# Every third weight unit gets its low part from an accumulating DMA instead of a VectorE subtraction

## The chip, the cores and the metric

The kernel runs on one core of a Trainium2 chip. The metric is the device time in microseconds of one execution; lower is better. Of the kernel before there are three runs, with a median of 2090.06 us (2090.04 to 2090.12).

## The reference

A two-layer decoder trunk on 256 tokens of 2048 features, all in float32. Layer 0 mixes by causal pooling, layer 1 by dilated attention; each is followed by a gated convolutional FFN of width 5504 and by layer norms. Cut to what matters here, it is a long row of matrix products with large weights and few tokens:

```python
# layer 0
p = h @ w_in                                  # 2048 x 2048
mixed = einsum('bsgc,gcd->bsgd', pooled, w_grp) * scale
h = layer_norm(ALPHA * h + mixed @ w_out)
h = layer_norm(ALPHA * h + conv_ffn(h))       # w_up 2048 x 11008, w_down 5504 x 2048
# layer 1
k, v, q = h @ w_k, h @ w_v, h @ w_q           # 2048 x 2048 each
h = layer_norm(ALPHA * h + attention(q, k, v) @ w_o)
h = layer_norm(ALPHA * h + conv_ffn(h))
```

## The kernel before

Each float32 weight is used as the sum of two numbers of a shorter format (float32r, which TensorE multiplies faster): a high part, the weight rounded, and a low part, the weight less its high part. The activations are split in the same way. A product is then w_high x_high + w_high x_low + w_low x_high, three products that TensorE sums in PSUM.

The weights are cut into 364 **units**, blocks of up to 512 rows by 512 columns, which lie in SBUF as 128 partitions x 2048 floats (1 MiB); 24 units of the FFNs have 384 columns or 384 rows. The list `units` sets the order of everything: `run_units` takes one unit after the other, emits its products, and before them calls `ahead(i)`, which issues loads up to unit i + 5 and splits up to unit i + 3. So a unit is split three units before TensorE uses it.

A unit goes through three kinds of buffers:

- `raw`, three buffers: the weights as SP's DMA queue loads them (line 68). The buffers turn round, so unit i uses buffer i mod 3. SP takes its queue in order, and a load waits until its buffer is free.
- `wh`, four buffers: the high part, written by ScalarE (line 76).
- `wl`, four buffers: the low part, written by VectorE as raw less wh (line 77).

The `wh` and `wl` of unit i + 4 can be written when TensorE is done with unit i. The products that read them stand at lines 135 and 136 (a mode with both halves of a PSUM bank), 138 to 140 (a mode with one half) and 164 to 166 (tokens on the partitions). ScalarE and VectorE also carry the products out of PSUM and do the convolution, the gating, the attention's softmax and the norms; their instructions run in the order in which the program emits them. GpSimd (POOL) has almost nothing to do: some memsets, the DMAs of the small constants (lines 792 to 798) at about 26 to 35 us, and three iotas for the attention's masks.

The first four units are split piece by piece, as their rows arrive.

Of the kernel before, what the change touches and what calls it, by code (L numbers as in the profile page):

```python
# [12 lines left out]
AF = mybir.ActivationFunctionType  # L13
OP = mybir.AluOpType
# [18 lines left out]
def trunk(ctx: ExitStack, tc: tile.TileContext, x, pool_w_in, pool_w_grp, pool_scale, pool_w_out,  # L33
          attn_w_q, attn_w_o, shared_w_k, shared_w_v, ffn_w_up, ffn_conv_w, ffn_conv_b, ffn_w_down,
          ln1_g, ln1_b, ln2_g, ln2_b, out):
    nc = tc.nc
    V, A, PE = nc.vector, nc.scalar, nc.tensor
# [10 lines left out]
    def bank(nm):  # L48
        return psp.tile([P, 512], F32, name=nm, tag="ps")

# [1 line left out]
    units = []  # L52
    state = {"loaded": 0, "split": 0, "done": 0}
    raw, wh, wl = {}, {}, {}
    pending, before = [], {}

    def pieces(i, nk):
        return [slice(k, k + 1) for k in range(nk)] if i < 4 else [slice(0, nk)]
# [11 lines left out]
    def do_split(i):  # L70
        r = raw.pop(i)
        shape = [P, r.shape[1], r.shape[2]]
        wh[i] = wp.tile(shape, F32R, name=f"wh{i}", tag="wh")
        wl[i] = wp.tile(shape, F32R, name=f"wl{i}", tag="wl")
        for j, s in enumerate(pieces(i, r.shape[1])):
            A.copy(wh[i][:, s], r[:, s])  # L76
            V.tensor_tensor(wl[i][:, s], r[:, s], wh[i][:, s].bitcast(F32), OP.subtract)  # L77
            if i == 0 and j == 0:
                x_quad(0, (1,))
# [32 lines left out]
                post()  # L112
            state["done"] += 1

# [1 line left out]
    # "ab": w xl beside the rest, in the second half of the bank; "a": all in the first half;  # L116
    # "x": two more columns, the products with the next norm's scale and shift
    XW = T + 2

    def mm_quad(xq, ps, first, last, mode, mid, shifted):  # L120
# [31 lines left out]
                          mm_quad(xqs[j], ps, j == 0, last, mode, mids[j] if j < len(mids) else None, shifted),  # L152
                          (lambda: post(ps)) if last else None))

    # the same product with tokens on the partitions; apart: all of the first 128 tokens first
    def group_tm(w, r0s, c0, ncol, xqs, post, apart=False):
        ps, held = [], []

# [58 lines left out]
    xsrcs = [lambda j=j: XC[j] for j in range(4)]  # L217
    psrcs = [lambda j=j: XP[j] for j in range(4)]

# [1 line left out]
    # d = residual sum less an estimate of its mean; the first product after the norm takes g*d in place of  # L221
    # the norm's result ("x" mode) and is corrected for mean and deviation as it leaves PSUM
    def resid_add(c, first):
        def post(ps):
            for m in range(4):
                y = H[c][:, m, :]
                if first:
                    V.scalar_tensor_tensor(y, y, ALPHA, ps[m][:, :T], op0=OP.mult, op1=OP.add)
                else:
                    V.tensor_tensor(y, y, ps[m][:, :T], OP.add)  # L230
            for m in range(4):
                y = H[c][:, m, :]
                V.tensor_tensor(y, y, ps[m][:, T:], OP.add)
        return post
# [132 lines left out]
                later(2 + q, lambda q=q: norm(q + 1))  # L367
            later(3 + q, lambda q=q: lo(q))

    # a group in "x" mode: (acc - mean * w g) * rstd + w b into dst(m)  # L370
    def norm_evac(ps, nb, tmp, dst):
        wgb = lnp.tile([P, 4, 2], F32, name="wgb", tag="wgb", bufs=2)
        for m in range(nb):
            A.copy(wgb[:, m, :], ps[m][:, T:XW])
        for m0 in range(0, nb, 2):
            ts = [(m, tmp()) for m in range(m0, min(nb, m0 + 2))]
            for m, t in ts:
                V.tensor_tensor(t, ps[m][:, :T], ST["rs"], OP.mult)
            for m, t in ts:
                V.scalar_tensor_tensor(t, ST["mr"], wgb[:, m, 0:1], t, op0=OP.mult, op1=OP.subtract)  # L380
                A.activation(dst(m), t, AF.Identity, scale=-1.0, bias=wgb[:, m, 1:2])

    # the first two column groups of a product take turns, so that its last rows are needed later
    def turns(mark, n):
        a, b = units[mark:mark + n], units[mark + n:mark + 2 * n]
        units[mark:mark + 2 * n] = a[:n - 1] + b[:1] + a[n - 1:] + b[1:]
# [6 lines left out]
        for c in range(4):  # L393
            group(w, rows, 512 * c, 512, srcs, resid_last(c, first, lay, which, after), mode="a", shifted=c > 0 and not first)

    # ================= layer 0, pooling mixer =================
    PADW = 16
    pooled_q, mixed_q = {}, {}

# [39 lines left out]
    def x_quad(q, halves=(0, 1)):  # L439
        xin = XIN  # L440
        if halves[0] == 0:
            H[q] = hp.tile([P, 4, T], F32, name="h", tag="h")
            XC[q] = quad_tile("xc")
        for half in halves:
            ps = bank("xT")
            for kk in range(2):
                for t in range(2):
                    k = 2 * half + kk
                    PE.transpose(ps[:, kk * T + t * P:kk * T + t * P + P], xin[q, t][:, k * P:(k + 1) * P], ident)
            pv2 = ps.rearrange("p (k t) -> p k t", k=2)  # L450
            s = slice(2 * half, 2 * half + 2)
            A.copy(XC[q][:, s, 0, :T], pv2)
            V.tensor_tensor(XC[q][:, s, 1, :T], pv2, XC[q][:, s, 0, :T].bitcast(F32), OP.subtract)
            before.setdefault(min(q + 1, 3), []).append(lambda s=s, pv2=pv2: A.copy(H[q][:, s, :], pv2))
# [22 lines left out]
    units.extend([outs[2], outs[4], outs[3]] + outs[5:])  # L477
    marks.append(len(units))

    # ================= FFN =================  # L480
    def ffn(lay):
        w_up, w_dn = ffn_w_up[lay], ffn_w_down[lay]
        gq, gates = {}, {}
# [101 lines left out]
                up(q)  # L585
            down(range(a, b), b == 11)

# [1 line left out]
    HT = {}  # L589

    def to_tokens(q):
# [54 lines left out]
    ffn(0)  # L646
    marks.append(len(units))

    # ================= layer 1, dilated attention =================
    scale = 1.0 / math.sqrt(P)  # L650
    qk, pr, oq, pT, vts = {}, {}, {}, {}, {}

# [92 lines left out]
    ffn(1)  # L745
    marks.append(len(units))

    # ================= the program =================
    with tc.tile_pool(name="start", bufs=1) as stp:
        for q in range(NQ):  # L750
            for t in range(2):
                XIN[q, t] = stp.tile([P, 512], F32, name=f"xin{q}{t}")
            halves = [slice(0, 256), slice(256, 512)] if q == 0 else [slice(0, 512)]
            for i, h in enumerate(halves):
                for t in range(2):
                    nc.sync.dma_start(XIN[q, t][:, h], x[0, t * P:(t + 1) * P, 512 * q:512 * q + 512][:, h])
                if q == 0:
                    do_load(0, i)
            if q in (1, 2):
                do_load(q)  # L760
            if q < 3:
                state["loaded"] = q + 1
            if q == 0:
                make_identity(nc, ident)
                V.memset(one1, 1.0)
                # the tensor engine's clock rises only under load: keep it busy until the first data is there
                warm = bank("warm")
                for i in range(WARM):
                    PE.matmul(warm[:, :P], one1, one1, start=True, stop=True)
        V.memset(ones, 1.0 / D)  # L770
        A.activation(neg1, one1[0:1, :], AF.Copy, scale=-1.0)
        A.activation(ones4, one1, AF.Copy, scale=4.0 / D)
        V.memset(epst, EPS)
        for c in range(16):
            nc.gpsimd.memset(inv[:, :, c:c + 1], 1.0 / (c + 1))
        x_quad(0, (0,))
        warm = bank("warm")
        for i in range(WARM2):
            PE.matmul(warm[:, :P], one1, one1, start=True, stop=True)

        run_units(3)
    with tc.tile_pool(name="pool", bufs=1) as pp:
# [5 lines left out]
        for l in range(2):  # L788
            n = 80 if l == 0 else 64
            r = pp.tile([80, P], F32, name=f"vrow{l}")  # L790
# [33 lines left out]
    with tc.tile_pool(name="ffn0", bufs=4) as fp:  # L824
        pools["ffn"] = fp

        # how many branches hold a (query, key) pair: keys 0-127 of both query tiles, keys 128-255 of the second
        def masks(i):
            dist = fp.tile([P, P], F32, name="dist", tag="dist", bufs=1)
            nc.gpsimd.iota(dist, pattern=[[-1, P]], base=P * (i == 1), channel_multiplier=1,  # L830
                           allow_small_or_imprecise_dtypes=True)
            idist = fp.tile([P, P], I32, name="idist", tag="idist", bufs=1)
            im = fp.tile([P, P], I32, name="im", tag="im", bufs=1)
            fm = fp.tile([P, P], F32, name="fm", tag="fm", bufs=1)
            cn = cnt[:, i, :]
            V.tensor_copy(idist, dist)
            V.tensor_scalar(cn, dist, float(P), None, op0=OP.is_le)
            for dil in (4, 16):
                V.tensor_scalar(im, idist, dil - 1, None, op0=OP.bitwise_and)
                V.tensor_copy(fm, im)  # L840
                V.scalar_tensor_tensor(cn, fm, 0.0, cn, op0=OP.is_equal, op1=OP.add)
            V.scalar_tensor_tensor(cn, dist, 0.0, cn, op0=OP.is_ge, op1=OP.mult)
            V.tensor_scalar(negm[:, i, :], cn, 0.0, NEG, op0=OP.is_equal, op1=OP.mult)

        for i in range(3):
            later(30 + 2 * i, lambda i=i: masks(i))
        run_units(marks[1])
# [35 lines left out]
```

## Time and profile before

| | |
|---|---|
| median of three runs | 2090.06 us |
| span of the profiled execution | 2086.0 us |
| difference of the two | 4.06 us |
| TensorE busy | 2071.3 us |
| VectorE busy, of it low parts (line 77) | 1393.2 us, 821.9 us |
| ScalarE busy, of it high parts (line 76) | 1030.2 us, 685.7 us |
| bytes read from HBM | 380.01 MB |

The profiled execution's own time is its span; the runs' times also hold the few microseconds around it. In the profile PE is TensorE's products, PEld its loads of weights into the array, DVE is VectorE, ACT is ScalarE, POOL is GpSimd and SP is the engine that issues the loads; SPq and POOLq are the queues that issue DMAs. A row of a group gives line, engine, operation, what is written and read, how many instructions, their busy time and mean duration, and the idle time of the engine just before them with what ended it. A row of the waits gives who waited for whom: total, times, longest. A row of stretches gives the stretch and its length, the busy time of PE, PEld, DVE, ACT and POOL with the instructions in parentheses, the granted clock of TensorE, the share of the DMA engines' time that was busy, and GB/s. An issue row gives the size of one transfer and the median time from issue to landing.

### The profile page before, as it was taken

To read this page: it belongs to the slowest core of one execution; us is meant where nothing else is said; L and a number is where in the kernel's file an instruction comes from. 1 tells how busy PE (TensorE), PEld (TensorE's weight loads), DVE (VectorE), ACT (ScalarE), POOL (GpSimd) and SP (SyncE) were. 2 spreads that over 40 slices of the span, in tenths; PEclk is the share of its full clock that TensorE was granted. 3 is DMA by queue.
4 is the path that set the end of the run, shared out by engine and by line. 5 is a ranking of instruction groups with operands and counts; after the bars stand their busy time and mean duration, and the time that the engine had idled before them with its cause. 6 is when DMAs were issued, how large, how long until landed. Compare 5 with 4: busy or idle time off the path is not lost.

```text
span 2086.0 us, 30530 instructions
## 1 busy us (share of the span) xinstructions
PE 2071.3 (99%) x12959; PEld 1862.8 (89%) x12959; DVE 1393.2 (67%) x1706; ACT 1030.2 (49%) x1146; POOL 11.4 (1%) x38
## 2 busy tenths in 40 slices
PE   9999999999999999999999999999999999999997
PEld 9999998888888888899888889999888888888886
DVE  6757787757756766767855666677646664675676
ACT  6445665345534535546634444476535543544553
POOL 2000000000000000000000000000000000000000
PEclk9999999999999999999999999999999999999999
DMA  8655465555555555554545445545555555555453
GB/s 265 212 187 188 148 212 174 201 184 191 172 200 186 178 202 172 188 186 143 201 161 182 161 162 182 185 159 194 190 184 187 195 182 192 191 182 188 165 197 136
DMA packets 195304, 384.09 MB, mean 184 GB/s; under 512 B 7022, under 2 KB 15876, under 8 KB 194912
## 3 DMA queue, kind: packets, MB, share of 16 engines
q1 hardware_dynamic: 194240, 381.71, 53.8%
q8 instruction: 101, 1.65, 0.3%
q0 software_dynamic: 928, 0.44, 0.1%
q14 instruction: 35, 0.29, 0.0%
HBM read 380.01 MB, written 2.10 MB: 183 GB/s over the span
## 4 chain that ended last, share of the span: by engine, by line
PE 99%; DVE 0%; DMA 0%; SPq 0%; issue 0%; DVEq 0%; ACT 0%
PE acc L135 35%; PE acc L136 18%; PE acc L138 9%; PE acc L139 9%; PE acc L140 9%; PE t L164 5%; PE t L166 5%; PE t L165 5%; PE s L693 0%; PE o L733 0%; DMA xin<-in_x_dram 0%; DVE ht L633 0%; PE pT L720 0%; PE acc L142 0%; PE o L734 0%; PE s L692 0%
## 5 line engine op out<-in xcount | busy, mean ns | idle before, releaser
L77 DVE TENSOR_TENSOR wl<-raw,wh 128x2048 fp32r<-128x2048 f32 (+2 forms) x376 | 821.9, 2188 | 537.0 <-ACT wh L76 526.0
L76 ACT CAST wh<-raw 128x2048 fp32r<-128x2048 f32 (+2 forms) x376 | 685.7, 1827 | 612.8 <-PE acc L135 297.8
L135 PE MATMUL acc<-xc,wh 128*128 128x512 f32 x2624 | 924.1, 396 | 0.0
L136 PE MATMUL acc<-xc,wl 128*128 128x256 f32 x2624 | 737.4, 281 | 0.0
L135 PEld LDWEIGHTS acc<-xc,wh 128*128 128x128 f32 x2624 | 495.3, 189 | 115.9
L136 PEld LDWEIGHTS acc<-xc,wl 128*128 128x128 f32 x2624 | 495.7, 189 | 0.2
L135 PE MATMUL acc<-g,wh 128*128 128x512 f32 x512 | 179.9, 396 | 0.0
L138 PE MATMUL acc<-xc,wh 128*128 128x256 f32 x512 | 144.8, 283 | 1.1 <-ACT wh L76 1.1
L140 PE MATMUL acc<-xc,wl 128*128 128x256 f32 x512 | 144.6, 282 | 0.2 <-DVE wl L77 0.2
L139 PE MATMUL acc<-xc,wh 128*128 128x256 f32 x512 | 144.3, 282 | 0.0
L136 PE MATMUL acc<-g,wl 128*128 128x256 f32 x512 | 143.8, 281 | 0.0
L518 DVE SCALAR_TENSOR_TENSOR c<-u,cv,c 128x256 f32<-128x256 f32 x344 | 141.9, 479 | 0.7
L164 PE MATMUL t<-wh,g 128*128 128x512 f32 x344 | 136.2, 396 | 0.0
L165 PE MATMUL t<-wl,g 128*128 128x512 f32 x344 | 135.6, 394 | 0.0
L166 PE MATMUL t<-wh,g 128*128 128x512 f32 x344 | 135.5, 394 | 0.0
L135 PEld LDWEIGHTS acc<-g,wh 128*128 128x128 f32 x512 | 96.7, 189 | 22.7
L139 PE MATMUL acc<-xp,wh 128*128 128x258 f32 x384 | 109.3, 285 | 0.0
L138 PE MATMUL acc<-xp,wh 128*128 128x258 f32 x384 | 109.2, 284 | 0.0
L140 PE MATMUL acc<-xp,wl 128*128 128x258 f32 x384 | 108.1, 281 | 0.0
L505 ACT COPY ut<-acc 128x256 f32<-128x256 f32 x140 | 51.6, 372 | 96.3 <-PE acc L136 96.1
L138 PEld LDWEIGHTS acc<-xc,wh 128*128 128x128 f32 x512 | 97.3, 190 | 1.3 <-ACT wh L76 1.3
L140 PEld LDWEIGHTS acc<-xc,wl 128*128 128x128 f32 x512 | 96.5, 189 | 0.5 <-DVE wl L77 0.4
(192 smaller groups left out, 2810.7 us busy)
## 6 DMA issues: line engine op xcount, KB each, us to landing
raw<-in_ffn_w_up_dram SPq DMA_DIRECT2D x160, 1024.0 KB, 4.8
raw<-in_ffn_w_down_dram SPq DMA_DIRECT2D x80, 1024.0 KB, 5.0
raw<-in_pool_w_out_dram SPq DMA_DIRECT2D x16, 1024.0 KB, 5.0
raw<-in_shared_w_k_dram SPq DMA_DIRECT2D x16, 1024.0 KB, 4.9
raw<-in_attn_w_q_dram SPq DMA_DIRECT2D x16, 1024.0 KB, 5.0
raw<-in_shared_w_v_dram SPq DMA_DIRECT2D x16, 1024.0 KB, 5.0
raw<-in_attn_w_o_dram SPq DMA_DIRECT2D x16, 1024.0 KB, 5.0
raw<-in_pool_w_in_dram SPq DMA_DIRECT2D x12, 1024.0 KB, 5.4
```

The lines of the kernel that those rows point to most:

```text
L76: A.copy(wh[i][:, s], r[:, s])
L77: V.tensor_tensor(wl[i][:, s], r[:, s], wh[i][:, s].bitcast(F32), OP.subtract)
L135: PE.matmul(ps[m], h[:, k, c], q[:, k, :, :T], start=st, stop=False)
L136: PE.matmul(ps[m][:, :T], l[:, k, c], q[:, k, 0, :T], start=False, stop=sp)
L138: PE.matmul(ps[m][:, :n], h[:, k, c], q[:, k, 0, :n], start=st, stop=False)
L139: PE.matmul(ps[m][:, :n], h[:, k, c], q[:, k, 1, :n], start=False, stop=False)
L140: PE.matmul(ps[m][:, :n], l[:, k, c], q[:, k, 0, :n], start=False, stop=sp and not shifted)
L164: PE.matmul(ps[t], xh, h[:, k, :], start=j == 0 and k == 0, stop=False)
L165: PE.matmul(ps[t], xh, l[:, k, :], start=False, stop=False)
L166: PE.matmul(ps[t], xl, h[:, k, :], start=False, stop=j == len(r0s) - 1 and k == nk - 1)
L505: A.copy(t, ps[m][:, T:])
L518: V.scalar_tensor_tensor(c[:, m, :], u[:, m, i:i + T], cv[:, i, j:j + 1], c[:, m, :], op0=OP.mult, op1=OP.add)
```

## The change

In `do_split`, units from 4 on whose number can be divided by 3 (6, 9, ... 363: 120 units) take another way. ScalarE first writes the negated rounding of the raw weights into `wl`, then the rounding into `wh`. GpSimd's queue then issues a DMA that reads the raw weights from SBUF and adds them to what stands in `wl`, also in SBUF: wl = raw - rounded(raw). The VectorE subtraction of these units is gone. The other 244 units are split as before. Comments were also taken out, and lines after the edit are six further down.

```diff
@@ -72,6 +72,12 @@
         shape = [P, r.shape[1], r.shape[2]]
         wh[i] = wp.tile(shape, F32R, name=f"wh{i}", tag="wh")
         wl[i] = wp.tile(shape, F32R, name=f"wl{i}", tag="wl")
+        if i >= 4 and i % 3 == 0:
+
+            A.activation(wl[i], r, AF.Copy, scale=-1.0)
+            A.copy(wh[i], r)
+            nc.gpsimd.dma_start(wl[i], r, accum_op=OP.add)
+            return
         for j, s in enumerate(pieces(i, r.shape[1])):
             A.copy(wh[i][:, s], r[:, s])
             V.tensor_tensor(wl[i][:, s], r[:, s], wh[i][:, s].bitcast(F32), OP.subtract)
```

What stands on ScalarE at one place of layer 0's FFN, in the down-projection, before (the number behind a name is that of its buffer in the built program):

```order
L76 CAST wh_5641<-raw_5536 128x2048
L199 CAST g<-c 128x4x256
L76 CAST wh_5687<-raw_5574 128x2048
L76 CAST wh_5725<-raw_5639 128x2048
L76 CAST wh_5767<-raw_5685 128x2048
L76 CAST wh_5813<-raw_5723 128x2048
```

and the same units on ScalarE in the changed kernel:

```order
L77 ACTIVATE wl_5673<-raw_5567 128x2048
L78 CAST wh_5672<-raw_5567 128x2048
L205 CAST g<-c 128x4x256
L82 CAST wh_5719<-raw_5605 128x2048
L82 CAST wh_5757<-raw_5670 128x2048
L77 ACTIVATE wl_5800<-raw_5717 128x2048
L78 CAST wh_5799<-raw_5717 128x2048
L82 CAST wh_5846<-raw_5755 128x2048
```

Every third unit now has two instructions on ScalarE, the negated one first; nothing else has changed places.

SP's loads of the same units before, with the semaphores that each waits for (DMAHW is an earlier transfer of SP's own, DVE is VectorE):

```order
L68 DMA raw_5536<-in_ffn_w_down_dram 128x4x512 [waits DMAHW6_49,DVE_49]
L68 DMA raw_5574<-in_ffn_w_down_dram 128x4x512 [waits DMAHW7_49,DVE_49]
L68 DMA raw_5639<-in_ffn_w_down_dram 128x4x512 [waits DMAHW0_49,DVE_49]
L68 DMA raw_5685<-in_ffn_w_down_dram 128x4x512 [waits DMAHW1_49,DVE_49]
L68 DMA raw_5723<-in_ffn_w_down_dram 128x4x512 [waits DMAHW2_49,DVE_49]
```

and in the changed kernel (DMASW is a transfer that GpSimd issued):

```order
L68 DMA raw_5567<-in_ffn_w_down_dram 128x4x512 [waits DMAHW6_49,DMASW3_49,Activation_49]
L68 DMA raw_5605<-in_ffn_w_down_dram 128x4x512 [waits DMAHW7_49,DVE_49]
L68 DMA raw_5670<-in_ffn_w_down_dram 128x4x512 [waits DMAHW0_49,DVE_49]
L68 DMA raw_5717<-in_ffn_w_down_dram 128x4x512 [waits DMAHW1_49,DMASW4_49,Activation_49]
L68 DMA raw_5755<-in_ffn_w_down_dram 128x4x512 [waits DMAHW2_49,DVE_49]
```

The order of the loads is the same; every third one now waits for GpSimd's transfer and for ScalarE, where it waited for VectorE, because these release the raw buffer.

## The prediction

> **What bounds the kernel now.** I read the engines' busy time first, then the clock and the stretches, then the chain of waits and the list of waits, and last the order of time inside one steady stretch.
>
> ```profile
> span 2086.0 us, 30530 instructions
> PE 2071.3 (99%) x12959; PEld 1862.8 (89%) x12959; DVE 1393.2 (67%) x1706; ACT 1030.2 (49%) x1146; POOL 11.4 (1%) x38
> ...
> PE 99%; DVE 0%; DMA 0%; SPq 0%; issue 0%; DVEq 0%; ACT 0%
> ...
> 100.00:300.00 200.00, 200.00 (x1681) 200.00 (x1681) 144.37 (x165) 111.39 (x141) 0.24 (x1) 1.00 0.53 180
> ...
> 1800.00:2086.00 286.00, 274.26 (x1415) 232.62 (x1414) 186.08 (x216) 131.31 (x134) 0.00 (x0) 0.98 0.51 176
> ```
>
> TensorE is the bound: 2071.3 of 2086.0 us busy, 99% of the chain that ended last, and in the stretch from 100 to 300 us it has no gap at a granted clock of 1.00. Its 14.7 idle us lie at the two ends: 11.7 of them in the last 286 us. The subtraction that the change moves is off this path:
>
> ```profile
> L77 DVE TENSOR_TENSOR wl<-raw,wh 128x2048 fp32r<-128x2048 f32 (+2 forms) x376 | 821.9, 2188 | 537.0 <-ACT wh L76 526.0
> ...
> DVE wl L77 <- ACT wh L76: 526.0, 249, 5.4
> ACT wh L76 <- PE acc L135: 297.8, 90, 4.1
> ...
> PEld acc L138 <- ACT wh L76: 1.3, 1, 1.3
> ...
> L77 DVE TENSOR_TENSOR wl<-raw,wh x376: 628/2292/2297, 5.9 to 2056.3; 128x2048 fp32r<-128x2048 f32 x170, 128x1536 fp32r<-128x1536 f32 x10, 128x512 fp32r<-128x512 f32 x8
> ```
>
> VectorE waits for ScalarE's rounding, ScalarE waits for TensorE to free a buffer, and TensorE waited for a split weight only at the start, for 1.3 us. So less work on VectorE buys nothing on the path. What the change can do is make TensorE wait. Whether it does is decided by two lead times, which the order of time in a steady stretch of layer 0's FFN shows (start, duration, and in brackets the idle time before and what ended it):
>
> ```profile
> 423.97 1.92 ACT L76 CAST wh<-raw 128x2048 fp32r<-128x2048 f32 x1 [3.69 <-PE acc L135]
> 429.58 1.91 ACT L76 CAST wh<-raw 128x2048 fp32r<-128x2048 f32 x1 [3.69 <-PE acc L135]
> 435.19 1.91 ACT L76 CAST wh<-raw 128x2048 fp32r<-128x2048 f32 x1 [3.70 <-PE acc L135]
> 440.81 1.91 ACT L76 CAST wh<-raw 128x2048 fp32r<-128x2048 f32 x1 [3.71 <-PE acc L135]
> ...
> 425.92 2.29 DVE L77 TENSOR_TENSOR wl<-raw,wh 128x2048 fp32r<-128x2048 f32 x1
> ...
> 428.24 0.37 SPq L68 DMA_DIRECT2D raw<-in_ffn_w_up_dram  x1
> ...
> DMA to landing us min/median/max: 4.8/4.9/5.0
> ```
>
> A unit takes TensorE 5.61 us (429.58 less 423.97), three take 16.83 (440.81 less 423.97). Each rounding starts the moment TensorE frees a buffer, three units ahead of its use. The raw buffer is free when the subtraction ends (425.92 + 2.29 = 428.21), SP issues the next load at 428.24, it lands 4.9 us later at 433.1, and the buffer's next rounding is at 440.81. So a load has **7.7 us** to spare, and a finished low part some 16.83 - (428.21 - 423.97) = **12.6 us**.
>
> **What the change removes.** Units 6, 9, ... 363 are changed, 120 of 364. VectorE loses 120 subtractions of 2.19 us (L77's mean), 263 us. TensorE is never behind them, so this is worth 0. The last subtraction starts at 2056.3 us, ahead of the norm at the end, which runs as before: worth 0 too.
>
> **What it adds on ScalarE.** 120 negated roundings of 1.91 us each, 229 us, on an engine that is 49% busy. Bounds per unit: 0 (ScalarE idles 3.7 us before such a rounding) and 1.91. They are covered by that idle time, except where the new chain below runs through them.
>
> **What it adds as a chain.** Three raw buffers turn round, and the changed units are every third: all of them use the same buffer. Its turn was load 4.9, rounding 1.9, subtraction 2.3. It becomes: load, negated rounding, POOL's issue, accumulating transfer. Only when that has landed may SP issue the next load into the buffer, and SP's queue is in order, so the next two loads stand behind it. If this turn is longer than 16.83 us, TensorE waits for the rest, each time. The terms:
>
> ```profile
> L76 ACT CAST wh<-raw x376: 617/1909/1962, 5.1 to 2054.8; 128x2048 fp32r<-128x2048 f32 x170, 128x1536 fp32r<-128x1536 f32 x10, 128x512 fp32r<-128x512 f32 x8
> ...
> 448.63 2.08 ACT L514 ACTIVATE c<-u,cv 128x256 f32<-128x256 f32 x4
> ...
> 28.11 0.49 POOL L794 DMA_DIRECT2D vrow<-in_pool_scale_dram  x1
> 28.59 1.88 POOL L797 DMA_DIRECT2D crow<-in_ffn_conv_w_dram  x1
> 30.47 0.55 POOL L798 DMA_DIRECT2D crow<-in_ffn_conv_b_dram  x1
> ...
> q1 hardware_dynamic: 194240, 381.71, 53.8%
> ...
> raw<-in_ffn_w_up_dram SPq DMA_DIRECT2D x160, 1024.0 KB, 4.8
> ...
> raw<-in_ffn_w_up_dram SPq DMA_DIRECT2D x16, 768.0 KB, 4.2
> ...
> crow<-in_ffn_conv_w_dram POOLq DMA_DIRECT2D x2, 129.0 KB, 11.5
> ```
>
> - Load: 4.9 us.
> - Negated rounding: 1.91 us, as the rounding of the same tile. The second, plain rounding runs beside the transfer.
> - Waiting behind other work in ScalarE's queue: 0 to 2.08 us, the longest group that stands next to a split; I take 0.3, since ScalarE idles before most.
> - POOL's issue: 0.49 us for 16 rows, 0.55 for 86, 1.88 for 258 pieces. The new transfer has 128 rows and has to name source and target; I take 1.88, nearest to 256 names.
> - The transfer itself, which no row of before shows: 1 MiB from SBUF added into SBUF. One load of 1 MiB keeps the 16 DMA engines for 0.538 x 2086.0 / 364 = 3.08 us (381.71 MB are 364 MiB), so 1.8 of its 4.9 us do not grow with size; 768 KB against 1024 KB gives 0.6 us per quarter, 2.4 per MiB, which agrees roughly. The lower end is a plain load's 4.9. The upper end is the slowest POOL-issued row, 11.5 for an eighth of the bytes, plus twice 3.08: 17.7, POOL's issue included. An accumulation has to read what it adds to as well, so I take double the bytes: 1.8 + 2 x 3.08 = 7.96 us.
> - Sharing the engines: when the turn is what limits, three loads leave at once and keep the engines for 9.24 us, while the new transfer starts some 9 us after them. I take 0.5; the bounds are 0 and 3.08, a whole load.
>
> Sum of one turn: 4.9 + 1.91 + 0.3 + 1.88 + 7.96 + 0.5 = **17.45 us**, against 16.83: TensorE would wait 0.62 us for every three units. This is a **knife edge**: the turn fits as soon as transfer and landing take under 7.34 us.
>
> The longer turn costs only where three units take no more than 16.83 us: both FFNs, 264 of 364 units (176 up, 88 down), 88 turns. Elsewhere TensorE has other products between the units. 88 x 0.62 = 55 us. The profiled execution's own time is its span, 2086.0, and 4.06 us around it up to the median of 2090.06; I keep the 4.06. 2090 + 55 = **2145 us**.
>
> The low part's own deadline is looser (1.91 + 0.3 + 1.88 + 7.96 = 12.1 of 16.83 us), so the buffer's turn decides, not the use. POOL's queue also holds three iotas, each behind a VectorE mask two units earlier in the program; they cost 0.
>
> **The skill beside the row.** The load's row alone, one read of 1 MiB, would make the transfer 4.9 us and the turn 14.4: no wait. The Trainium skill, in Collectives: The Full Stack, section The bandwidth ceiling: the fold count and why AG ≠ RS ≠ AR, says that an add in the DMA path is free as arithmetic but needs two source reads on one ring, and that a reduction therefore ran at about half a gather's rate; by that the turn is 17.45, and no run here has shown it yet. The Trainium skill's DMA: Bandwidth & Descriptors, section Where 436 GB/s comes from, gives 435 GB/s as the ceiling between SBUF and SBUF; two MiB at that rate are an estimated 4.8 us, the turn 16.1 us, and nothing would be lost, which is the result of rival 1.
>
> **The rivals.**
>
> 1. **No change.** The engines move data that stays in SBUF a tenth faster than data from HBM (5.54 us for two reads, not 6.16), or the second read overlaps the first, so that the transfer lands within 7.34 us, or POOL's issue is 0.55 us, not 1.88 (turn 16.1). From there on the 7.7 us of slack swallow everything: 2090 us. For it: TensorE's 99%, and a plain load that lands in 4.9. Against it: double bytes. Price 0; it decides at a turn of 16.83.
> 2. **The accumulating transfer is much slower than two loads**, because each row is read, added and written in steps, or POOL's issue is slow. At the upper end, a turn of 4.9 + 1.91 + 0.3 + 17.7 = 24.8 us, 8 us over, in about 119 turns: 2090 + 950 = 3040; halfway from the forecast, about 2590. For it: POOL-issued transfers took up to 11.5 us for 129 KB. Against it: those ran while the start's loads filled the engines.
> 3. **VectorE's relief shows.** It would have to shorten one of the two ends; those 14.7 us are loads and the last norm, no low part in them. At most 2086.
>
> **How the numbers follow.** Forecast (a turn slightly over, 2095 to 2300 us): 0.43, at 2145. No change: 0.37, at 2090. Much slower (over 2300): 0.17. Faster: 0.03. A measurement of this kernel tells about 0.2% (4 us) from no change, so faster 0.03, same 0.37, slower 0.60. The range takes in no change from below (2086) and reaches into rival 2 as far as a turn of about 22 us, 2700; some 0.1 lies above it.
>
> **What would show it.** Right: TensorE waiting on the transfer into wl at the first low-part product of every third unit, SP waiting for that transfer where it waited for VectorE, ScalarE waiting for a load, and the POOL-issued 1 MiB transfers landing in about 10 us from issue. The sum is wrong if they land in under 9 with TensorE at 99% (rival 1), or over 12 (rival 2). If the turn is long and TensorE still does not wait, my reading of the shared buffer is wrong.

## The result, and the profile after

The change made the kernel a little slower: 2101.79 us (median of 4 runs, 2099.68 to 2103.19) against 2090.05 us for the kernel before beside it. The ratio is 1.0062, with an interval of 1.0051 to 1.0074: 11.7 us. The forecast was 55 us slower; the direction held, the size did not, and the profile shows that the loss does not lie where the forecast put it.

The page of the changed kernel, in the parts shown of before: span, busy time, the DMA queues, and the chain by engine.

```profile
span 2098.8 us, 30899 instructions
PE 2075.0 (99%) x12959; PEld 1863.9 (89%) x12959; DVE 1137.6 (54%) x1586; ACT 1235.0 (59%) x1266; POOL 112.9 (5%) x158
q1 hardware_dynamic: 194240, 381.71, 52.7%
q0 software_dynamic: 18208, 123.92, 29.0%
PE 90%; DMA 6%; ACT 1%; issue 1%; DVE 1%; SPq 0%; POOL 0%; DVEq 0%; POOLq 0%; ACTq 0%
```

VectorE lost 256 us of work, ScalarE gained 205, and the 16 DMA engines, which were some 54% busy, are now 82% busy, 29 points of it by GpSimd's transfers. TensorE is still the bound. What its products waited for, in the list of waits:

```profile
PE acc L146 <- DMA wl<-raw: 7.1, 3, 5.0
PE t L171 <- DMA wl<-raw: 1.9, 1, 1.9
```

Not 88 waits of 0.6 us, but **four waits** in all, 9.0 us together, one of them 5.0 us long. They account for most of the change: the span grew by 12.8 us (2098.8 less 2086.0), of which 9.0 are these waits, and TensorE's busy time for the same products grew by another 3.7 (2075.0 less 2071.3). The transfers themselves, by the issue rows, and the waits of SP's queue:

```profile
raw<-in_ffn_w_up_dram SPq DMA_DIRECT2D x160, 1024.0 KB, 5.6
wl<-raw POOLq DMA_DIRECT2D x111, 1024.0 KB, 7.7
...
SPq L68 <- DMA wl<-raw: 1342.2, 119, 16.3
SPq L68 <- DVE wl L83: 327.4, 89, 8.8
```

SP does wait for the new transfer at every changed unit, 119 times, as the order of the program had said. But the transfer lands 7.7 us after GpSimd begins to issue it, where the forecast's sum had 10.3. One **turn** of the raw buffer, from one load into it to the next, in layer 0's FFN, from the order of time on SP, ScalarE and POOL:

```profile
441.21 0.37 SPq L68 DMA_DIRECT2D raw<-in_ffn_w_up_dram  x1
...
448.58 1.92 ACT L77 ACTIVATE wl<-raw 128x2048 fp32r<-128x2048 f32 x1 [3.82 <-PE acc L142]
...
450.79 0.85 POOL L79 DMA_DIRECT2D wl<-raw  x1 [15.96 <-ACT wl L77]
...
457.73 0.37 SPq L68 DMA_DIRECT2D raw<-in_ffn_w_up_dram  x1
```

The load leaves at 441.21. The negated rounding at 448.58 waited for TensorE's buffer, not for the load: the weights had been there for some 2 us (loads of this stretch land in 5.3 us). The transfer has landed by 457.73, when the buffer's next load leaves. So of the 16.5 us from load to load some 2 are slack, and TensorE sets the pace. At the first of the four places it is otherwise:

```profile
40.12 0.92 POOL L79 DMA_DIRECT2D wl<-raw  x1 [4.56 <-DMA crow<-in_ffn_conv_b_dram]
...
51.66 0.58 PE L146 MATMUL acc<-xc,wl 128*128 128x256 f32 x1 [5.02 <-DMA wl<-raw]
...
40.00:50.00 10.00, 6.64 (x58) 6.44 (x56) 5.63 (x8) 5.02 (x7) 0.92 (x1) 0.96 0.95 222
50.00:60.00 10.00, 8.34 (x53) 8.14 (x54) 2.29 (x1) 5.07 (x3) 0.84 (x1) 0.70 0.75 263
```

This is unit 6, the first changed one. Its transfer leaves at 40.12 and TensorE goes on at 51.66, 11.5 us later; the DMA engines are 95% busy from 40 to 50 us (last but one column), with the loads that fill the pipeline, with the small DMAs of the constants and with this transfer itself. TensorE comes to this low part at 46.6, only 6.5 us after the transfer left. It waits 5.0 us. During the wait, at 49.2, the granted clock falls to half, and it stays there until 56.0 (the 0.70 of the second stretch is the mean; the column before the DMA share). The other three, the first of them at the end of layer 0's FFN:

```profile
877.52 0.37 SPq L68 DMA_DIRECT2D raw<-in_ffn_w_down_dram  x1
...
869.53 1.48 ACT L77 ACTIVATE wl<-raw 128x1536 fp32r<-128x1536 f32 x1
...
882.73 1.92 ACT L77 ACTIVATE wl<-raw 128x2048 fp32r<-128x2048 f32 x1 [3.54 <-DMA raw<-in_ffn_w_down_dram]
...
884.94 0.85 POOL L79 DMA_DIRECT2D wl<-raw  x1 [12.79 <-ACT wl L77]
...
893.54 0.39 PE L146 MATMUL acc<-g,wl 128*128 128x256 f32 x1 [0.56 <-DMA wl<-raw]
...
1405.50 1.91 ACT L77 ACTIVATE wl<-raw 128x2048 fp32r<-128x2048 f32 x1
...
DMA to landing us min/median/max: 11.6/11.6/11.6
...
1419.35 0.38 PE L146 MATMUL acc<-xc,wl 128*128 128x256 f32 x1 [1.55 <-DMA wl<-raw]
...
2068.77 1.49 ACT L77 ACTIVATE wl<-raw 128x1536 fp32r<-128x1536 f32 x1 [6.16 <-DMA raw<-in_ffn_w_down_dram]
...
2077.29 0.50 PE L171 MATMUL t<-wl,g 128*128 128x512 f32 x1 [1.86 <-DMA wl<-raw]
```

At about 893 us units of 384 columns (128 x 1536) pass, which TensorE finishes in three quarters of the time; now ScalarE waits for the load, the turn runs without slack, and TensorE waits 0.56 us for its end. The other two places are in layer 1. At 1419 us, the start of its FFN, the unit is of full size, but ScalarE came to its negated rounding straight from the work of the norm (no idle time ahead of it), so the transfer left at 1407.7, some 10 us before TensorE came to this low part, and it took 11.6 us to land (the row between). At 2077 us, among the last products, short units pass again, and ScalarE waited 6.2 us for the load.

### The profile page after: what moved, and what is told of

It is laid out like the page before. It is cut to its first block, busy times and chain, and to the rows that moved or that the text cites. A ratio compares the mean times of both kernels' runs of the same rounds, so it can differ in the third digit from the quotient of the medians.

```text
span 2098.8 us, 30899 instructions
## 1 busy us (share of the span) xinstructions
PE 2075.0 (99%) x12959; PEld 1863.9 (89%) x12959; DVE 1137.6 (54%) x1586; ACT 1235.0 (59%) x1266; POOL 112.9 (5%) x158
## 4 chain that ended last, share of the span: by engine, by line
PE 90%; DMA 6%; ACT 1%; issue 1%; DVE 1%; SPq 0%; POOL 0%; DVEq 0%; POOLq 0%; ACTq 0%
PE acc L141 34%; PE acc L142 17%; PE acc L144 8%; PE acc L146 8%; PE acc L145 8%; PE t L170 4%; PE t L171 4%; PE t L172 4%; DMA wl<-raw 4%; DMA raw<-in_ffn_w_down_dram 1%; DMA crow<-in_ffn_conv_w_dram 1%; DMA raw<-in_ffn_w_up_dram 0%; PE s L699 0%; PE o L739 0%; DMA xin<-in_x_dram 0%
## 5 line engine op out<-in xcount | busy, mean ns | idle before, releaser
L83 DVE TENSOR_TENSOR wl<-raw,wh 128x2048 fp32r<-128x2048 f32 (+2 forms) x256 | 551.9, 2160 | 522.8 <-ACT wh L82 514.3
L82 ACT CAST wh<-raw 128x2048 fp32r<-128x2048 f32 (+2 forms) x256 | 460.1, 1803 | 270.3 <-PE acc L141 128.7
L141 PEld LDWEIGHTS acc<-xc,wh 128*128 128x128 f32 x2624 | 495.0, 189 | 116.6
L142 PEld LDWEIGHTS acc<-xc,wl 128*128 128x128 f32 x2624 | 494.8, 189 | 0.2
L77 ACT ACTIVATE wl<-raw 128x2048 fp32r<-128x2048 f32 (+1 forms) x120 | 226.2, 1885 | 266.4 <-PE acc L142 109.1
L78 ACT CAST wh<-raw 128x2048 fp32r<-128x2048 f32 (+1 forms) x120 | 223.0, 1858 | 0.0
L79 POOL DMA_DIRECT2D wl<-raw x120 | 101.5, 846 | 1933.6 <-ACT wl L77 1484.1
```

The source lines that it names most:

```text
L77: A.activation(wl[i], r, AF.Copy, scale=-1.0)
L78: A.copy(wh[i], r)
L141: PE.matmul(ps[m], h[:, k, c], q[:, k, :, :T], start=st, stop=False)
L142: PE.matmul(ps[m][:, :T], l[:, k, c], q[:, k, 0, :T], start=False, stop=sp)
```

## The experiments

Four theories were set against each other. A: the loss is made at four places without lead, above all at unit 6, while the steady stretches cost nothing, because the raw buffer's turn is shorter than the 16.8 us of three units. B: the transfers bleed the kernel evenly. C: the start's wait only moves to another unit. D: the buffer's turn is no limit at all. Each run is compared with runs of the kernel before on the same chip, whose medians were 2088.4 us there.

**Unit 6 back to VectorE.**

```diff
-        if i >= 4 and i % 3 == 0:
+        if i >= 9 and i % 3 == 0:
```

> Only unit 6 goes back to the VectorE subtraction; the other 119 units stay changed. Theory A (the loss is made at four places where the split has no lead, 7.7 us of it at unit 6; in the steady stretches a turn of the raw buffer takes about 15.2 us of 16.8 and costs nothing): 7 to 8 us less than the changed kernel, about 2094, and no TensorE wait near 52 us. Theory B (the transfers bleed the kernel evenly, through busy DMA engines or more work on ScalarE): at most 0.1 us less, about 2102. Theory C (the start only moves: the first changed unit, now 9, waits in place of 6): 2100 to 2102, with a wait near 60 us.

Measured: 2093.58 us against 2088.42, ratio 1.0023 (1.0014 to 1.0032), so 5.2 us above before where the full change was 11.7 above. The wait near 52 us is gone, and the next changed unit brings no wait in its place; the other three stay, and one of 0.2 us at 1430 us is new:

```profile
PE acc L146 <- DMA wl<-raw: 2.9, 3, 1.8
PE t L171 <- DMA wl<-raw: 1.8, 1, 1.8
```

119 changed units cost 5 us, one cost 6 to 7. C falls, and so does B as the whole account. Whether the 5 us that are left are spread evenly is decided by the third experiment.

**Unit 6 alone.**

```diff
-        if i >= 4 and i % 3 == 0:
+        if i == 6:
```

> Unit 6 alone is changed, the other 119 are split as before. Theory A: this one unit of 364 costs 7 to 8 us, about 2097.5, with one TensorE wait of some 5 us near 52 us and a granted clock well under 1 in the 10 us behind it. Theory B: 0.1 us, about 2090.1. Theory C: as A.

Measured: 2095.95 us against 2088.42, ratio 1.0036 (1.0023 to 1.0049): **one transfer costs 7.5 us**. The stretches with the wait and behind it, and the wait, which lasts from 46.7 to 52.3:

```profile
40.00:50.00 10.00, 6.70 (x58) 6.49 (x57) 5.70 (x8) 5.35 (x7) 0.91 (x1) 0.97 0.97 221
50.00:60.00 10.00, 7.72 (x48) 7.53 (x49) 2.88 (x2) 3.81 (x3) 0.00 (x0) 0.69 0.71 244
60.00:70.00 10.00, 10.00 (x86) 10.00 (x87) 7.45 (x6) 5.87 (x9) 0.00 (x0) 1.00 0.85 289
...
PE acc L146 <- DMA wl<-raw: 5.6, 1, 5.6
```

It landed 11.9 us after its issue, with no other transfer of its kind in the kernel, so a queue of such transfers did not hold it up. At first the 16 engines were full (97% busy from 40 to 50 us), with SP's loads and with the small DMAs of the constants, which GpSimd's queue had issued just before; towards the end, from 49.4 to 52.2 us, they were only 19% busy. Which of the two kinds held it up, and why its end took so long, no run separates.

**The four places left out.**

```diff
-        if i >= 4 and i % 3 == 0:
+        if i >= 9 and i % 3 == 0 and not (147 <= i <= 159 or 237 <= i <= 246 or i >= 351):
```

> Changed units are left out where the changed kernel's TensorE waited: unit 6, units 147 to 159, 237 to 246 and from 351 on; some 106 of 120 stay changed. Theory A: nothing is lost, 2090 (2089 to 2091.5), with no TensorE wait on a transfer. Theory B: 106 of 120 parts of the loss stay, about 2100. If it is between, waits have moved to other places, and the profile names them.

Measured: 2088.39 us against 2088.42, ratio 0.9998 (0.9989 to 1.0007). No product of TensorE waits for a transfer any more (one load of weights does, for 0.2 us), though 105 units are still split by DMA and VectorE has 227 us less to do than before:

```profile
PE 2071.8 (99%) x12959; PEld 1862.1 (89%) x12959; DVE 1166.1 (56%) x1601; ACT 1212.2 (58%) x1251; POOL 100.2 (5%) x143
```

So the whole loss, within some 2 us, lies in those places, and the relief of VectorE is worth nothing that can be measured. B falls. This is the best version found; it is not faster than before.

**The turn made longer by one rounding.** The plain rounding goes ahead of the negated one, so the transfer leaves 1.9 us later.

```diff
-            A.activation(wl[i], r, AF.Copy, scale=-1.0)
             A.copy(wh[i], r)
+            A.activation(wl[i], r, AF.Copy, scale=-1.0)
```

> In the changed units the plain rounding stands ahead of the negated one, so each transfer leaves 1.9 us later; the work is the same. Theory A with the buffer's turn as the limit: the turn goes from about 15.2 to 17.1 us against 16.8, so TensorE waits some 0.3 us in each of the 88 turns of the FFNs and no delay is caught up again: 2120 to 2170, with many waits of TensorE on the transfer and loads that land just before ScalarE takes them. Theory D (the turn is no limit, only the low part's own lead of 16.8 us less some 12 counts): 1.9 us more at the start and at the three other places, 2102 to 2110. Theory B: no change, 2102.

Measured: 2107.27 us, ratio 1.0086 (1.0072 to 1.0100): by its numbers D, and A missed. TensorE waits for a transfer in nine places, 14.0 us in all. The order of time shows why the two were not yet apart:

```profile
485.25 0.37 SPq L68 DMA_DIRECT2D raw<-in_ffn_w_up_dram  x1
...
490.28 1.91 ACT L77 CAST wh<-raw 128x2048 fp32r<-128x2048 f32 x1 [3.57 <-DMA raw<-in_ffn_w_up_dram]
492.09 1.91 ACT L78 ACTIVATE wl<-raw 128x2048 fp32r<-128x2048 f32 x1
...
501.78 0.37 SPq L68 DMA_DIRECT2D raw<-in_ffn_w_up_dram  x1
...
DMA to landing us min/median/max: 6.9/7.0/8.7
```

ScalarE now waits for the load in the steady stretch too, so the turn holds no slack any more, and it takes 16.53 us (501.78 less 485.25), just under 16.83. (In the changed kernel the distance was the same, but some 2 us of it were slack.) The transfer, pushed later, lands in 7.0 us (median from 430 to 800 us), where it took 7.4 in the changed kernel in the same stretch; that gave back part of the 1.9 us. Why it lands earlier was not tested.

**The turn made longer by two roundings.** As above, and the plain rounding is written twice.

```diff
+            A.copy(wh[i], r)
             A.copy(wh[i], r)
+            A.activation(wl[i], r, AF.Copy, scale=-1.0)
```

> As with the plain rounding first, and that rounding is written twice, so each transfer leaves another 1.9 us later. The run before it showed a turn of 16.0 to 18.2 us, just at the 16.8 that three units take. Theory A with the buffer's turn as the limit: now 18.0 to 19, over the edge; TensorE waits 1.2 to 2 us in nearly every turn of the FFNs (88) and some elsewhere: 2200 to 2330, with tens of waits on the transfer. Theory D (no limit by the turn; each delay is paid only at the rough places): 5 us more than with the rounding first, 2108 to 2115.

Measured: 2204.32 us, ratio 1.0562 (1.0544 to 1.0580), 116 us above before, and waits of TensorE on the transfer in 38 places:

```profile
506.25 0.37 SPq L68 DMA_DIRECT2D raw<-in_ffn_w_up_dram  x1
525.95 0.37 SPq L68 DMA_DIRECT2D raw<-in_ffn_w_up_dram  x1
...
PE 2105.6 (96%) x12959; PEld 1881.5 (85%) x12959; DVE 1128.1 (51%) x1586; ACT 1446.4 (66%) x1386; POOL 112.9 (5%) x158
...
PE acc L147 <- DMA wl<-raw: 34.2, 13, 7.0
PE acc L143 <- DMA wl<-raw: 25.2, 16, 2.8
PE t L172 <- DMA wl<-raw: 18.5, 9, 4.6
```

The same 1.9 us that cost 7 us at the first step (18.9 above before, against 11.7) cost 97 at the second, and the waits stand in the steady stretches too. So D falls, and the account with an edge at 16.83 us fits: the turn shown takes 19.70 us. It is one of the long ones; between 397 and 854 us the transfers leave 17.6 us apart in the mean, against 16.8 in the changed kernel (400 to 855 us).

The run does not show the edge cleanly, though, because the raw buffers no longer turn round strictly in it. The transfer ahead of those shown left at 502.40 and landed 7.9 us later, at 510.3. The next changed unit's load left at 506.25, without waiting for it: it went into a buffer that VectorE had just released, and the load behind it, at 510.33, waited for the transfer. By the semaphores of SP's loads this is so in 52 of 118 places (10 of 119 with the rounding first, none in the changed kernel). A changed unit whose load need not wait can be a reason for 38 waits in place of 88. How much of the 97 us is due to the longer turn and how much to the other order of the buffers is not shown.

**A plain copy in place of the addition.** The low part of the changed units is then the raw weights, so the output is not the reference's.

```diff
-            nc.gpsimd.dma_start(wl[i], r, accum_op=OP.add)
+            nc.gpsimd.dma_start(wl[i], r)
```

> GpSimd's transfer copies the raw weights over wl and adds nothing, so the low part of the changed units is wrong by the high part. It measures the price of the second read. If the add costs a second read of the bytes at the engines' pace (prediction: 3.08 us more per MiB), the transfer lands in 4.5 to 5.5 us from issue, not 7.7, and the queue's share of the engines falls from 29% to about 17%. If SBUF to SBUF is simply fast and the second read overlaps, it lands in 7 to 7.7 as before. The time: the wait at unit 6 shrinks by the shorter landing, so 2094 to 2098 by the first, 2101 by the second.

Measured: 2093.53 us, ratio 1.0026 (1.0015 to 1.0037), and one wait, at unit 6, of 3.4 us. That is the first account, a little under its numbers. The queue and the issue row, and how long POOL issues:

```profile
q0 software_dynamic: 18208, 123.92, 15.4%
...
wl<-raw POOLq DMA_DIRECT2D x111, 1024.0 KB, 4.3
...
L79 POOL DMA_DIRECT2D wl<-raw x120: 528/531/566, 39.4 to 2062.1; - x120
```

120 transfers are 117.75 MiB. The copy keeps the engines for 0.154 x 2091.7 / 117.75 = 2.74 us per MiB, the addition for 0.290 x 2098.8 / 117.75 = 5.17. The second read is real and costs 2.4 us of the engines, 0.3 of POOL's issue (0.85 against 0.53) and 3.4 until landing. The other three waits are gone with it, so at those places too it is the longer way of the addition that uses up the lead.

**Every second unit.**

```diff
-        if i >= 4 and i % 3 == 0:
+        if i >= 9 and i % 2 == 0:
```

> From unit 10 on every second unit is changed, not every third (177 units), so the raw buffers take turns in holding a transfer, and 1.5 times as many bytes are added by DMA. By the engines: loads 52.7% and transfers 29.0% x 1.5 = 43.5% give 96% busy. If the engines' time is the next limit (theory A, edge at 100%): waits of TensorE on transfers in many places, landing times of 9 us and more, 2110 to 2200. If only the buffer's turn counted, each buffer now has six units for two loads and one transfer, and 2094 to 2100 would remain.

Measured: 2280.67 us, and 2328.61 in a second run, slower than either theory had it. TensorE waits on transfers 66 times, for 106 us; transfers and loads both land in 8.6 us:

```profile
q1 hardware_dynamic: 194240, 381.71, 48.8%
q0 software_dynamic: 26416, 183.43, 41.2%
...
wl<-raw POOLq DMA_DIRECT2D x167, 1024.0 KB, 8.6
raw<-in_ffn_w_up_dram SPq DMA_DIRECT2D x160, 1024.0 KB, 8.6
```

The engines are 90% busy over the whole span, and 96% from 430 to 800 us, where TensorE is busy for 352 of the 370 us. So their time is a candidate for the loss. SP's in-order queue behind the transfers, which now hold all three buffers in turn, is the other; the two were not separated.

## Why the prediction was right or wrong

- **TensorE is the bound, VectorE's relief is worth 0**: right. With the four places out, VectorE did 227 us less and the ratio was 0.9998.
- **The shared raw buffer's turn, with an edge at 16.83 us**: right as a mechanism. SP waited for the transfer 119 times, and a turn of 16.5 us without slack made no wait in the steady stretch shown, while the next 1.9 us brought waits in 38 places and 97 us. That the edge lies at 16.83 us fits these two runs, but the second also changed the order of the buffers, so it is not shown alone.
- **The terms of the sum were mis-sized, and this is the step that failed.** POOL's issue, transfer and sharing were put at 1.88 + 7.96 + 0.5 = 10.34 us; the median from issue to landing is 7.7. POOL's issue is 0.85 us, not 1.88: the row of 258 pieces was the wrong neighbour. The doubling of the bytes was right in kind (5.17 against 2.74 us, a factor of 1.89) but started from a load's 3.08 us, while a copy inside SBUF takes 2.74. The Trainium skill's Collectives: The Full Stack, section The bandwidth ceiling: the fold count and why AG ≠ RS ≠ AR, with its two source reads, agrees with this factor; the estimate of 4.8 us from DMA: Bandwidth & Descriptors of the Trainium skill, section Where 436 GB/s comes from, came nearer to the measured 5.17 than the forecast's 6.16. With 7.7 the forecast's own sum is 4.9 + 1.91 + 0.3 + 7.7 = 14.8 us, below the edge: rival 1's side for the steady stretch. The loads went the other way, 5.6 us beside the transfers in place of 4.9; with them it is 15.5, still below. Two small readings of the forecast were off and change nothing: 440.81 less 423.97 is 16.84 us, not 16.83, and the 11.5 us of the slowest row that GpSimd issued are the median of two, the longest of these small DMAs being 12.0.
- **The forecast spread the loss over 88 turns of the FFNs, and rival 1 had none at all.** Both read the slack from a steady stretch and applied it everywhere. The 11.7 us lie where that slack does not exist: 6.5 to 7.5 at the first changed unit, while the pipeline of loads is filling, and the rest at three places (about 893, 1419 and 2077 us). At 893 and 2077 the trace shows short units, at 1419 a rounding that stands behind the norm's work and a landing of 11.6 us. That these are what takes the slack is read from the trace and was not tested place by place. Tested is that the loss goes when the units there are split as before, and that the three waits go when the transfer lands in 4.3 us.
- **The low part's own deadline**, which the forecast had as the looser one (12.1 of 16.83 us), held in the steady stretches and failed at unit 6, where TensorE was 6.5 us behind the transfer's issue and the landing took 11.5. The forecast's direction held partly by luck: waits in every turn of the FFNs, which it was added up from, did not occur, and the loss comes from places that stood in none of its terms.

## What to carry to other kernels

Moving work off an engine that nobody waits for cannot gain time, but it can spend the slack of the one that feeds the bound; so look at how long a buffer is held, not at how busy the engines are. Work out the slack of such a turn at the worst places as well as in a steady stretch: at the first use, in short tiles and at stage borders, where a single late transfer cost more than the other 119. Near an edge the cost is not proportional: here 1.9 us more per turn cost 7 us in one step and 97 in the next, though the second step also changed the order of the buffers.

## What the hardware showed that was not expected

- **A wait costs more than itself.** With unit 6 alone changed, TensorE waited 5.6 us and the kernel lost 7.5. The granted clock fell to half 2.7 us into the wait and stayed there until 56.2 us: behind the wait 18 products took 3.9 us, where just after that 31 took 3.7. So some 1.8 us more were lost behind the wait. With the plain rounding written twice, 77.9 us of waits cost 116, and TensorE's busy time for the same products rose from 2071.3 to 2105.6 us. How long a wait must be is not plain. In that run, a wait of 1.78 us that ended at 636.1 was followed by half the clock, and one of 3.26 us that ended at 1815.3 was not (stretches as before, the clock is the column ahead of the DMA share):

```profile
632.00:636.20 4.20, 2.42 (x14) 1.83 (x13) 4.20 (x8) 0.00 (x0) 0.00 (x0) 1.00 0.96 186
636.30:639.60 3.30, 3.30 (x12) 2.83 (x12) 0.66 (x2) 0.58 (x1) 0.00 (x0) 0.50 1.07 405
639.70:643.00 3.30, 3.30 (x20) 2.86 (x19) 0.00 (x0) 3.27 (x3) 0.00 (x0) 1.00 1.03 384
...
1815.30:1822.00 6.70, 6.70 (x29) 5.46 (x30) 1.38 (x2) 3.96 (x3) 0.00 (x0) 1.00 1.05 395
```

  The Trainium skill's TensorE: Matmul & The Clock Gate, section Part 1: The HAM clock gate, has the clock fall to half after at least one idle window of about 3.4 us that runs free of the kernel. The half agrees, and so does a window of that length: in the clock's records of this run each stretch at half clock but the last takes 3.41, 6.83 or 10.24 us. But the 1.78 us do not fit an idle window of that length, and the measurement decides.
- **The time until an accumulating transfer lands varies widely**: for 1 MiB it was 6.9 us at best in the changed kernel (430 to 800 us), 7.7 in its median, and 11.9 with unit 6 alone changed, where the engines were 97% busy from 40 to 50 us.
